# Two transformer blocks on one core: stacked queries and keys in the mixers, a new order of their steps, and row copies by transposes

## The chip, the core and the metric

The kernel runs on one core of one Trainium2 chip. The metric is the device time of one execution in microseconds (us). TensorE (PE in the rows) multiplies 128x128 weight blocks with moving data, VectorE (DVE) and ScalarE (ACT) work element by element, SyncE (SP) issues the loads. Two kernels whose times differ by less than about 0.2% (5 us) can't be told apart by the measurement here.

## The reference

256 tokens of width 1024, float32, pass through a first block of two layers (neighbourhood attention, grouped attention, feed-forward) and a second block of two layers (feed-forward, hybrid mixer, feed-forward). The change is mostly in the hybrid mixer:

```python
def hybrid_mixer(h, ...):
    (q_a, k_a, v_a, f_a, q_b, k_b, v_b, q_c, c_kv, q_i, k_i, w_i, gates) = jnp.split(h @ w_in, _split_points(), axis=-1)
    y_a = forgetting_attention(...)        # 6 "fox" heads of width 64
    y_b = stick_breaking_attention(...)    # 5 "stick" heads
    y_c = dsa_attention(...)               # 5 heads on the 64 best keys of a query, by an index score
    g_a, g_b, g_c = jnp.split(jax.nn.sigmoid(gates), N_BRANCH, axis=-1)
    merged = (g_a * (y_a @ w_up_fox) + g_b * (y_b @ w_up_sb) + g_c * (y_c @ w_up_dsa))
    return merged @ w_out
```

The stick heads need a sum over all later keys before their exponent, so a head is a chain: score, log terms, a second product, exponent, product with the values. The index score of a query goes through relu and a weighted sum, and its 64 largest keys are kept.

## The kernel before, in words

Activations stand transposed: features on the 128 partitions, 256 tokens along the columns. Every float32 operand is split into a high part (`hi`, an ACT instruction of L403) and a low part (`lo`, DVE, L408 or L409), and a product is three matmuls: high by high, high by low, low by high. Nearly all of them are issued at L427. Weights come in by SyncE in pieces of 512 KB, and each piece is split into `hwmx` and `lwmx` (mixers), 512 columns to a buffer, in eight pairs of buffers. The scheduler of the language turns the program into one fixed order for each engine; each engine works through its own in that order and waits where an operand isn't there.

The mixers' program order is a table, `MIX_ORDER`. `K` makes the keys, queries and values that all heads share; `S0` to `S2` and `F0` to `F2` are the projections of the stick and fox heads; `s0` to `s4`, `x0` to `x5` and `d0` to `d5` are the heads; `T0` and `T1` score the index keys of a query block and find the 64 best (eight rounds of MAX and MATCH_REPLACE on DVE, L1568 and L1569); `G` tokens are the gates' projections, `A`, `B` and `C` the ways up (`mix_up`) for fox, stick and dsa heads.

A head is 64 wide, and so are the contractions of its scores: `scores` (L731, fox and dsa heads and the index) and the first products of `stick_head` (L1647) multiply operands on 64 partitions. In the profile a matmul of 64 rows reads `64*128`, one of 128 rows `128*128`. The last of the three chunks of `B` and `C` is 64 rows, too (`n = HD`):

```python
for n, (a, b) in enumerate(((0, 0), (0, 1), (1, 0))):
    nc.tensor.matmul(out, q[a], k[b], start=start and n == 0, stop=stop and n == 2, skip_group_check=True)
```

`rows` (L542) and `b1_keys` (L928) bring a column or row of numbers onto all partitions by a float32 matmul with the identity. `sums` (L486) uses a transpose for a like step.

Of the kernel before, what the change touches and what calls it, by code (L numbers as in the profile page):

```python
# [8 lines left out]
F32 = mybir.dt.float32  # L9
# [113 lines left out]
def _h(base, *hs):  # L123
# [13 lines left out]
MIX_ORDER = (  # L137
    "K S0 T0 F0 s0 s1 S1 T1 S2 s2 s3 G1 G10 x0 F2 F1 s4 G4 G8 x2 G5 B3 x3 d2 G0 d0 G2 G11 x1 d1 G9 x4 x5 d3 d4 d5 A0 G7 B2 G3 B1".split()
)
# [54 lines left out]
def pieces(n, kparts):  # L194

    most = RAW // n // (SUB // n) * (SUB // n)
    return [min(most, nk - k) for nk in kparts for k in range(0, nk, most)]
# [169 lines left out]
class Builder:  # L367
# [171 lines left out]
    def rows(self, ps, r):  # L539

        for t in range(2):
            i = self.nc.tensor.matmul(  # L542
                ps[:, t * P : (t + 1) * P], r[:, t : t + 1].broadcast_to((P, P)), self.ident, start=True, stop=True
            )
        return i
# [157 lines left out]

    def stack_q(self, src, n, scale=1.0):


        t = self.ap_.tile([P, 2, n], F32R, tag="q2", name=self.u("q2"), bufs=2)
# [18 lines left out]

    def scores(self, out, q, k, start=True, stop=True):

        nc = self.nc
        for n, (a, b) in enumerate(((0, 0), (0, 1), (1, 0))):  # L730
            nc.tensor.matmul(out, q[a], k[b], start=start and n == 0, stop=stop and n == 2, skip_group_check=True)  # L731

# [181 lines left out]
    def b1_keys(self, l, w, full, cos, sin):  # L914
# [11 lines left out]
        for t in range(4):  # L926
            o = slice(t * P, (t + 1) * P)
            nc.tensor.matmul(pr[:, o], rw[:, o], self.ident, start=True, stop=True)  # L928
        nc.vector.tensor_tensor(kc, kc, pr, ALU.mult)
# [342 lines left out]
    def mixer(self, l):  # L1272
        w = Weights(self, f"wmx_{l}")
        hh, hl = self.h
        rsb = self.rsb[0]
        xs = lambda k: (hh[:, k], hl[:, k])
        with self.open(f"mo{l}") as op:
            yh = op.tile([P, 9, SEQ], F32R, name=f"yh2{l}")
            yl = op.tile([P, 9, SEQ], F32R, name=f"yl2{l}")
            gates = {}  # L1280
            with self.open(f"ma{l}", "right") as self.ap_:
                run = self.mix_attention(l, w, hh, hl, xs, rsb, yh, yl, op, gates)
            with self.open(f"mm{l}") as mp:
                self.mix_merge(w, run, mp, gates, self.p(f"gf2{l}"))
        assert w.off == w.ap.shape[0] and w.i == len(w.spec)
# [34 lines left out]
    def mix_attention(self, l, w, hh, hl, xs, rsb, yh, yl, op, gates):  # L1320
# [23 lines left out]
        for b in (b1, b2):  # L1344
            t = self.t2("rq")
            self.rope(pairs(t), pairs(b), twice(cr), twice(sr), SWAP2)
            h, lo = self.parts("cq", t, bufs=2)
            qs += [(h[:, :SEQ], lo[:, :SEQ]), (h[:, SEQ:], lo[:, SEQ:])]

# [32 lines left out]
        def query(n, cols):  # L1382

            o = slice(64 * ((n + 1) % 2), 64 * ((n + 1) % 2) + 64)
            return [a[o, cols] for a in qs[(n + 1) // 2]], o

# [4 lines left out]
        def keys(_):  # L1391
# [25 lines left out]
            self.rope(kv[64:, SEQ:], kv[64:, SEQ:], cos[64:], sin[64:], SWAP2)  # L1417
            qs[0] = self.parts("iq", kv[:, SEQ:], SEQ, bufs=1)

        def project(kind, n):  # L1420
            (b,) = self.product()
            wk = w.next()
            if kind == "S" and n == 2:
                self.group([(0, b[:, :SEQ], 0, P, None)], wk, range(NKT), xs)
                k4 = self.t2("k4")[:64, :SEQ]
                nc.scalar.copy(k4, b[64:, :SEQ])
                kt = [ap.tile([64, SEQ], F32R, tag=f"k{c}", name=self.u("k4"), bufs=3) for c in "hl"]
                self.hi(kt[0], k4)
                self.lo(kt[1], k4, kt[0])
                ready[kind, n] = self.parts("q", b[:, :SEQ], SEQ, HD**-0.5, bufs=3), kt  # L1430
                return
            self.group([(0, b[:, :SEQ], 0, P, None), (0, b[:, SEQ:], P, P, None)], wk, range(NKT), xs)
            ready[kind, n] = (
                self.parts("q", b[:, :SEQ], SEQ, HD**-0.5, bufs=3), self.parts("k", b[:, SEQ:], SEQ, bufs=3)
            )
# [5 lines left out]
        def out(i):  # L1441
            if i not in y32:
                y32[i] = ap.tile([P, SEQ], F32, tag="y32", name=self.u("y32"), bufs=3)
            return y32[i]

        def stick(h):
            q, k = ready["S", h // 2]
            o = slice(64 * (h % 2), 64 * (h % 2) + 64)
            y = out(3 + h // 2)
            self.stick_head(h, [a[o] for a in q], [a[o] for a in k], vs, y[o])  # L1450
            if h % 2 or h == 4:
                finish(3 + h // 2, y, P if h % 2 else HD)

        def fox(h):
            i, j = divmod(h, 2)
            if j == 0:
                ck[i] = self.forget_rows(ccol, h)
            q, k = ready["F", i]
            o = slice(64 * j, 64 * j + 64)
            y = out(i)  # L1460
            self.fox_head(h, [a[o] for a in q], [a[o] for a in k], vs, ck[i], j, y[o])
            if j:
                finish(i, y, P)
# [6 lines left out]
        def dsa(n):  # L1470
            hp, qb = divmod(n, 2)
            heads = DSA_HEADS[hp]
            y = out(6 + hp)
            self.dsa_pair(heads, qb, query, vs, masks[qb], y)
            if qb:
                finish(6 + hp, y, len(heads) * HD)
# [33 lines left out]
    def mix_up(self, w, b, yh, yl, g):  # L1510
# [4 lines left out]
        for k in range(3):  # L1515
            n = HD if (b and k == 2) else P
            wh, wl = wk(k)
            for a, y in ((wh, yh), (wh, yl), (wl, yh)):
                for j in range(2):
                    ops.append((0, j, bk[:, j * SEQ : (j + 1) * SEQ], a[:n, j * P : (j + 1) * P], y[:n, 3 * b + k]))  # L1520
        self.matmuls(ops)
# [25 lines left out]
    def index(self, qb, query, ik, fw):  # L1547
# [4 lines left out]
        for hp in range(2):  # L1552
            s = self.bank("s")
            for j in range(2):
                q, o = query(hp + 2 * j, slice(qb * P, (qb + 1) * P))
                self.scores(s[:, j * SEQ : j * SEQ + nk], q, [a[o, :nk] for a in ik])
            rl = self.t2("rl").rearrange("p (a t) -> p a t", a=2)
# [80 lines left out]
    def stick_head(self, h, q, k, vs, y32):  # L1638
# [34 lines left out]
    def dsa_pair(self, heads, qb, query, vs, mask, y32):  # L1673
# [136 lines left out]
```

## Time and profile before

| | us |
|---|---|
| median of 3 runs | 2501.16 (2499.57 to 2503.38) |
| the profiled execution | 2499.92 |
| its span, first to last instruction | 2498.1 |
| PE busy | 2440.1 (98%) |
| DVE busy | 1836.9 (74%) |
| ACT busy | 1373.1 (55%) |

The mixers run from about 1441 to 1682 us and from 2058 to 2300 us of the span. Durations of matmuls overlap: two that follow one another start 0.12 us apart at 256 columns though each lasts 0.28 us. What a matmul costs is therefore read from starts in the timeline, not from durations; the same holds for DVE, to a smaller degree.

### The profile page before, as it was taken

Reading aid. Unit: us, or ns where it says so; the run is one execution under the profiler, and the core shown is the slowest. Engines: PE = TensorE matmul, PEld = TensorE weight load, DVE = VectorE, ACT = ScalarE, POOL = GpSimd, SP = SyncE. Lnnn points to the kernel's source line nnn. Section 1 sums busy time; section 2 is a strip of 40 time slices with the busy share of each in tenths; the row PEclk is TensorE's granted clock in tenths of the full one; section 3 lists DMA queues with packets and bytes.
Section 4 is the critical chain, followed back from the end, with each engine's and each line's share of the span. In section 5 each row is a group of like instructions: output and inputs, shape, how many; then the busy total and the mean of one; then the engine's idle time right before and its main releaser. Section 6 shows DMA issues by size and latency. Waiting matters only on the chain.

```text
span 2498.1 us, 46101 instructions
## 1 busy us (share of the span) xinstructions
PE 2440.1 (98%) x17342; PEld 2257.4 (90%) x17342; DVE 1836.9 (74%) x4131; ACT 1373.1 (55%) x2683; POOL 0.2 (0%) x4
## 2 busy tenths in 40 slices
PE   8999999999999999999999999999999999999997
PEld 4877768888888898999999999999999999999997
DVE  6677886885766889876676687786666668778665
ACT  5566763422233667665555566755555556665553
POOL 0000000000000000000000000000000000000000
PEclk9999999999999999999999999999999999999999
DMA  7221453454654433565555553356666655336553
GB/s 265 92 72 56 147 178 137 159 184 141 208 183 135 127 115 106 155 187 182 182 185 182 184 182 109 113 178 186 181 186 186 183 180 184 100 116 190 184 180 102
DMA packets 112543, 393.46 MB, mean 157 GB/s; under 512 B 12480, under 2 KB 13760, under 8 KB 111808
## 3 DMA queue, kind: packets, MB, share of 16 engines
q1 hardware_dynamic: 112320, 390.52, 49.1%
q8 instruction: 136, 2.23, 0.4%
q14 instruction: 87, 0.71, 0.1%
HBM read 389.42 MB, written 1.05 MB: 156 GB/s over the span
## 4 chain that ended last, share of the span: by engine, by line
PE 95%; DVE 3%; ACT 2%; issue 0%; DMA 0%; SPq 0%; DVEq 0%; ACTq 0%
PE mm L427 84%; PE y L427 2%; PE s L427 2%; PE s L778 1%; PE y L785 1%; PE s L731 1%; PE y L542 1%; PE y L486 0%; PE mm L610 0%; PE y L678 0%; ACT nt L575 0%; DVE lwmx L408 0%; ACT k L403 0%; DVE kl L408 0%; DVE lwm L408 0%
## 5 line engine op out<-in xcount | busy, mean ns | idle before, releaser
L427 PE MATMUL mm<-hh,hwb 128*128 128x512 f32 (+2 forms) x1176 | 348.5, 341 | 2.6 <-ACT gt L1008 1.4
L427 PE MATMUL mm<-hl,hwb 128*128 128x512 f32 (+1 forms) x1176 | 347.5, 340 | 0.1
L427 PE MATMUL mm<-hh,lwb 128*128 128x512 f32 (+2 forms) x1176 | 347.0, 340 | 0.0
L403 ACT ACTIVATE hwb<-wb_0r 128x512 fp32r<-128x512 f32 (+1 forms) x250 | 149.6, 611 | 253.0 <-PE mm L427 243.5
L427 PE MATMUL mm<-gh,hwf 128*128 128x256 f32 x1344 | 269.5, 281 | 0.0
L427 PE MATMUL mm<-gh,lwf 128*128 128x256 f32 x1344 | 269.1, 281 | 0.0
L427 PE MATMUL mm<-gl,hwf 128*128 128x256 f32 x1344 | 268.4, 281 | 0.0
L408 DVE TENSOR_TENSOR lwf<-wf_1r,hwf 128x512 fp32r<-128x512 f32 (+1 forms) x272 | 183.4, 676 | 109.1 <-ACT hwf L403 100.1
L408 DVE TENSOR_TENSOR lwf<-wf_0r,hwf 128x512 fp32r<-128x512 f32 (+1 forms) x272 | 183.3, 675 | 102.9 <-ACT hwf L403 93.1
L403 ACT ACTIVATE hwf<-wf_1r 128x512 fp32r<-128x512 f32 (+1 forms) x272 | 168.2, 619 | 162.9 <-PE mm L427 149.3
L403 ACT ACTIVATE hwf<-wf_0r 128x512 fp32r<-128x512 f32 (+1 forms) x272 | 168.2, 619 | 162.2 <-PE mm L427 146.5
L427 PEld LDWEIGHTS mm<-hh,hwb 128*128 128x128 f32 x1176 | 204.0, 189 | 29.0 <-ACT gt L1008 2.4
L408 DVE TENSOR_TENSOR lwb<-wb_0r,hwb 128x512 fp32r<-128x512 f32 (+1 forms) x250 | 163.4, 665 | 86.2 <-ACT hwb L403 83.3
L427 PEld LDWEIGHTS mm<-hl,hwb 128*128 128x128 f32 x1176 | 203.7, 189 | 25.5 <-DVE hl L408 0.7
L427 PEld LDWEIGHTS mm<-hh,lwb 128*128 128x128 f32 x1176 | 204.1, 189 | 25.0
L403 ACT ACTIVATE hwb<-wb_1r 128x512 fp32r<-128x512 f32 (+1 forms) x242 | 146.2, 611 | 112.2 <-PE mm L427 101.6
L427 PEld LDWEIGHTS mm<-gh,hwf 128*128 128x128 f32 x1344 | 206.4, 188 | 0.0
L427 PEld LDWEIGHTS mm<-gh,lwf 128*128 128x128 f32 x1344 | 206.4, 188 | 0.0
L427 PEld LDWEIGHTS mm<-gl,hwf 128*128 128x128 f32 x1344 | 206.1, 188 | 0.0
L408 DVE TENSOR_TENSOR lwb<-wb_1r,hwb 128x512 fp32r<-128x512 f32 (+1 forms) x242 | 158.3, 666 | 63.2 <-ACT hwb L403 60.1
L427 PE MATMUL mm<-gl,hwmx 128*128 128x256 f32 x656 | 138.9, 289 | 3.3 <-DVE gl L408 3.3
L427 PE MATMUL mm<-actl,hwf 128*128 128x256 f32 x704 | 141.8, 283 | 0.0
(414 smaller groups left out, 5680.9 us busy)
## 6 DMA issues: line engine op xcount, KB each, us to landing
wf_0r<-in_wf_dram SPq DMA_DIRECT2D x120, 512.0 KB, 3.6
wf_1r<-in_wf_dram SPq DMA_DIRECT2D x120, 512.0 KB, 3.5
wb_0r<-in_wb_dram SPq DMA_DIRECT2D x108, 512.0 KB, 3.7
wb_1r<-in_wb_dram SPq DMA_DIRECT2D x105, 512.0 KB, 3.6
wmx_0r<-in_wmx_dram SPq DMA_DIRECT2D x49, 512.0 KB, 3.6
wmx_1r<-in_wmx_dram SPq DMA_DIRECT2D x49, 512.0 KB, 3.6
wm2r<-in_wm_dram SPq DMA_DIRECT2D x48, 512.0 KB, 3.5
wm1r<-in_wm_dram SPq DMA_DIRECT2D x24, 512.0 KB, 4.0
```

Source lines behind the costliest of these rows:

```text
L403: self.nc.scalar.activation(out, src, AF.Copy, scale=scale)
L408: return self.nc.vector.tensor_tensor(out, src, h, ALU.subtract)
L427: i = nc.tensor.matmul(out, lhsT, rhs, start=bank not in first, stop=n[bank] == 0, skip_group_check=True)
L542: i = self.nc.tensor.matmul(ps[:, t * P : (t + 1) * P], r[:, t : t + 1].broadcast_to((P, P)), self.ident, start=True, stop=True)
L731: nc.tensor.matmul(out, q[a], k[b], start=start and n == 0, stop=stop and n == 2, skip_group_check=True)
L778: nc.tensor.matmul(s[:, :nk], q[:, o], part, start=n == 0, stop=n == 1, skip_group_check=True)
L785: nc.tensor.transpose(tp[:, j * P : (j + 1) * P], pt[:, j * P : (j + 1) * P], self.ident)
```

## The change

Stacked scores: the query's high part goes on one half of the partitions and its low part on the other half; the key's high part is written to both halves of one buffer, its low part to both halves of another. A score is then two matmuls of 128 rows. The last chunk of `B` and `C` is multiplied over all 128 rows, and the unused half of `yh` and `yl` is set to zero once a mixer. `rows` and `b1_keys` call a transpose. `MIX_ORDER` is new: both `T` stand ahead of the stick heads, `G8` and `G9` earlier, and `B3` behind `x0` and ahead of `G5`. `out` tells a head whether it is the last of its chunk, so that heads can come in any order. The limits on buffers of queries and keys are 3 and 5.

```diff
--- before.py
+++ after.py
@@ -135,7 +135,7 @@
-    "K S0 T0 F0 s0 s1 S1 T1 S2 s2 s3 G1 G10 x0 F2 F1 s4 G4 G8 x2 G5 B3 x3 d2 G0 d0 G2 G11 x1 d1 G9 x4 x5 d3 d4 d5 A0 G7 B2 G3 B1".split()
+    "K S0 G8 T0 T1 F0 s0 S2 s1 S1 G1 G9 s3 G10 F1 s2 s4 x0 B3 G5 x2 G4 x1 d1 F2 x3 d0 G2 G0 G11 x4 x5 d2 d3 B1 G7 G3 d4 d5 A0 B2".split()
...
@@ -539,9 +539,7 @@
         for t in range(2):
-            i = self.nc.tensor.matmul(
-                ps[:, t * P : (t + 1) * P], r[:, t : t + 1].broadcast_to((P, P)), self.ident, start=True, stop=True
-            )
+            i = self.nc.tensor.transpose(ps[:, t * P : (t + 1) * P], r[:, t : t + 1].broadcast_to((P, P)), self.ident)
...
@@ -724,11 +722,27 @@
-    def scores(self, out, q, k, start=True, stop=True):
+    def stacked_q(self, out, src, a):
+        b = slice(64 - a.start, 128 - a.start)
+        self.hi(out[a], src[a])
+        self.lo(out[b], src[a], out[a])
+    def stacked_k(self, src, a, n):
+        b = slice(64 - a.start, 128 - a.start)
+        h, l = (self.ap_.tile([P, n], F32R, tag=f"k{c}", name=self.u(f"k{c}"), bufs=5) for c in "hl")
+        self.hi(h[a], src[a])
+        self.hi(h[b], src[a])
+        self.lo(l[a], src[a], h[a])
+        self.lo(l[b], src[a], h[a])
+        return h, l
+    def scores(self, out, q, k):
...
-        for n, (a, b) in enumerate(((0, 0), (0, 1), (1, 0))):
-            nc.tensor.matmul(out, q[a], k[b], start=start and n == 0, stop=stop and n == 2, skip_group_check=True)
+        for n, part in enumerate(k):
+            nc.tensor.matmul(out, q, part, start=n == 0, stop=n == 1, skip_group_check=True)
@@ -925,7 +939,7 @@
-            nc.tensor.matmul(pr[:, o], rw[:, o], self.ident, start=True, stop=True)
+            nc.tensor.transpose(pr[:, o], rw[:, o], self.ident)
@@ -1277,6 +1291,10 @@
+            for i in (5, 8):
+                for t in (yh, yl):
+                    self.nc.vector.tensor_copy(t[HD:, i], self.ident[HD:, 0:1].broadcast_to((HD, SEQ)))
@@ -1344,8 +1362,10 @@
-            h, lo = self.parts("cq", t, bufs=2)
-            qs += [(h[:, :SEQ], lo[:, :SEQ]), (h[:, SEQ:], lo[:, SEQ:])]
+            q = ap.tile([P, 2, 512], F32R, tag="cq", name=self.u("cq"), bufs=2)
+            for j in range(2):
+                self.stacked_q(q[:, j], t, slice(64 * j, 64 * j + 64))
+            qs += [q[:, :, :SEQ], q[:, :, SEQ:]]
...
@@ -1415,23 +1434,23 @@
-            qs[0] = self.parts("iq", kv[:, SEQ:], SEQ, bufs=1)
+            qs[0] = ap.tile([P, 2, SEQ], F32R, tag="iq", name=self.u("iq"), bufs=1)
+            self.stacked_q(qs[0][:, 1], kv[:, SEQ:], slice(64, 128))
...
-                k4 = self.t2("k4")[:64, :SEQ]
-                nc.scalar.copy(k4, b[64:, :SEQ])
-                kt = [ap.tile([64, SEQ], F32R, tag=f"k{c}", name=self.u("k4"), bufs=3) for c in "hl"]
-                self.hi(kt[0], k4)
-                self.lo(kt[1], k4, kt[0])
-                ready[kind, n] = self.parts("q", b[:, :SEQ], SEQ, HD**-0.5, bufs=3), kt
+                q = ap.tile([P, 2, SEQ], F32R, tag="q2", name=self.u("q4"), bufs=3)[:, 0]
+                self.hi(q[:64], b[:64, :SEQ], HD**-0.5)
+                self.lo(q[64:], b[:64, :SEQ], q[:64], HD**-0.5)
+                ready[kind, n] = [q], [self.stacked_k(b[:, :SEQ], slice(64, 128), SEQ)]
...
+            q = self.stack_q(b[:, :SEQ], SEQ, HD**-0.5, bufs=3)
...
-                self.parts("q", b[:, :SEQ], SEQ, HD**-0.5, bufs=3), self.parts("k", b[:, SEQ:], SEQ, bufs=3)
+                [q[:, j] for j in range(2)], [self.stacked_k(b[:, SEQ:], slice(64 * j, 64 * j + 64), SEQ) for j in range(2)]
@@ -1439,27 +1458,29 @@
         def out(i):
-            if i not in y32:
-                y32[i] = ap.tile([P, SEQ], F32, tag="y32", name=self.u("y32"), bufs=3)
-            return y32[i]
+            if i in y32:
+                return y32.pop(i), True
+            y32[i] = ap.tile([P, SEQ], F32, tag="y32", name=self.u("y32"), bufs=3)
+            return y32[i], i == 5
...
-            y = out(3 + h // 2)
-            self.stick_head(h, [a[o] for a in q], [a[o] for a in k], vs, y[o])
-            if h % 2 or h == 4:
-                finish(3 + h // 2, y, P if h % 2 else HD)
+            y, last = out(3 + h // 2)
+            self.stick_head(h, q[h % 2], k[h % 2], vs, y[o])
+            if last:
+                finish(3 + h // 2, y, P if h < 4 else HD)
...
-            if j == 0:
-                ck[i] = self.forget_rows(ccol, h)
+            if i not in ck:
+                ck[i] = self.forget_rows(ccol, 2 * i)
...
-            y = out(i)
-            self.fox_head(h, [a[o] for a in q], [a[o] for a in k], vs, ck[i], j, y[o])
-            if j:
+            y, last = out(i)
+            self.fox_head(h, q[j], k[j], vs, ck[i], j, y[o])
+            if last:
...
@@ -1513,11 +1534,10 @@
-            n = HD if (b and k == 2) else P
...
-                    ops.append((0, j, bk[:, j * SEQ : (j + 1) * SEQ], a[:n, j * P : (j + 1) * P], y[:n, 3 * b + k]))
+                    ops.append((0, j, bk[:, j * SEQ : (j + 1) * SEQ], a[:, j * P : (j + 1) * P], y[:, 3 * b + k]))
...
@@ -1644,7 +1664,7 @@
         for b, (o, kb, qs) in enumerate(((z[:, :SEQ], slice(0, P), slice(0, SEQ)), (z[:, SEQ:W], slice(P, SEQ), slice(P, SEQ)))):
-            ops += [(0, b, o, k[i][:, kb], q[j][:, qs]) for i, j in ((0, 0), (0, 1), (1, 0))]
+            ops += [(0, b, o, a[:, kb], q[:, qs]) for a in k]
...
```

On PE a fox head's score stood in the middle of a gate's projection like this (`s` is the score's bank, `mm` the projection):

```order
L427 MATMUL mm1928_18352<-gl1718_16112,hwmx_0_15_0_18334 128x256
L731 MATMUL s1893_18026<-kh1820_17536,qh1818_17532 128x128
L731 MATMUL s1893_18026<-kl1821_17537,qh1818_17532 128x128
L731 MATMUL s1893_18026<-kh1820_17536,ql1819_17533 128x128
L731 MATMUL s1893_18026<-kh1820_17536,qh1818_17532 128x256
L731 MATMUL s1893_18026<-kl1821_17537,qh1818_17532 128x256
L731 MATMUL s1893_18026<-kh1820_17536,ql1819_17533 128x256
L427 MATMUL mm1928_18352<-gl1718_16112,hwmx_0_15_0_18334 128x256
```

and now (L745 is the new line of `scores`):

```order
L427 MATMUL mm1944_18519<-gl1718_16112,hwmx_0_17_0_18501 128x256
L745 MATMUL s1911_18312<-kh1833_17664,q21832_17659 128x128
L745 MATMUL s1911_18312<-kl1834_17665,q21832_17659 128x128
L745 MATMUL s1911_18312<-kh1833_17664,q21832_17659 128x256
L745 MATMUL s1911_18312<-kl1834_17665,q21832_17659 128x256
L427 MATMUL mm1944_18519<-gl1718_16112,hwmx_0_17_0_18501 128x256
L427 MATMUL mm1944_18519<-gh1717_16111,lwmx_0_17_0_18502 128x256 x2
L427 MATMUL mm1944_18519<-gh1717_16111,hwmx_0_17_0_18501 128x256
```

Six matmuls became four, and they are as high as their neighbours.

On PE, while the first stick heads of the first mixer are under way, the program before has a projection (`mm`) around their matmuls (L1663 is a head's second product):

```order
L427 MATMUL mm1926_18281<-gh1717_16111,hwmx_0_14_4_18273 128x256
L1663 MATMUL s1867_17792<-ph1870_17807,stickr1740_16778 128x256
L1663 MATMUL s1867_17792<-ph1870_17807,stickr1741_16780 128x128
L1663 MATMUL s1867_17792<-ph1870_17807,stickr1740_16778 128x128
L427 MATMUL mm1926_18281<-gh1717_16111,hwmx_0_14_4_18273 128x256
L427 MATMUL mm1926_18281<-gl1718_16112,hwmx_0_14_4_18273 128x256
L1663 MATMUL s1867_17792<-pl1871_17808,stickr1740_16778 128x256
L1663 MATMUL s1867_17792<-pl1871_17808,stickr1741_16780 128x128
L1663 MATMUL s1867_17792<-pl1871_17808,stickr1740_16778 128x128
L427 MATMUL mm1926_18281<-gl1718_16112,hwmx_0_14_4_18273 128x256
L427 MATMUL mm1926_18281<-gh1717_16111,lwmx_0_14_4_18274 128x256 x2
L427 MATMUL mm1926_18281<-gh1717_16111,hwmx_0_14_4_18273 128x256 x2
```

Now, from the end of the projection of `F1` on, 32 rows hold matmuls of stick heads alone; these are the last of them and what comes next. `mm1924` is the way up `B3`, which reads `yh`, the finished output of the first two heads, and `mm1925` is the gate `G5`:

```order
L427 MATMUL y1858_17785<-ph1856_17781,vs21756_17025 128x256
L427 MATMUL y1858_17785<-pl1857_17782,vs21756_17025 128x256
L427 MATMUL y1858_17785<-ph1856_17781,vs21756_17025 128x128
L427 MATMUL y1858_17785<-pl1857_17782,vs21756_17025 128x128
L1683 MATMUL s1871_18024<-ph1874_18037,stickr1740_16782 128x256
L1683 MATMUL s1871_18024<-ph1874_18037,stickr1741_16784 128x128
L1683 MATMUL s1871_18024<-ph1874_18037,stickr1740_16782 128x128
L1683 MATMUL s1871_18024<-pl1875_18038,stickr1740_16782 128x256
L1683 MATMUL s1871_18024<-pl1875_18038,stickr1741_16784 128x128
L1683 MATMUL s1871_18024<-pl1875_18038,stickr1740_16782 128x128
L427 MATMUL mm1924_18358<-yh20_16769,hwmx_0_15_0_18350 128x256 x2
L427 MATMUL mm1925_18398<-gh1717_16111,hwmx_0_16_0_18380 128x256 x2
```

The projection that could be done meanwhile now stands behind a matmul that needs the heads.

On DVE, between the low part that the first head's second product reads (`pl1842`, which stands two rows ahead, with one weight split between) and the one that its product with the values reads (`pl1844`), there now stand the end of one search (`sc1803`), the beginning of the other (`sc1817`), weight splits and the doubled low keys (`kl`):

```order
L1588 MAX small1814_17536<-sc1803_17498 128x8
L408 TENSOR_TENSOR kl1863_17870<-mm1860_17795,kh1862_17869 64x256 x2
L408 TENSOR_TENSOR lwmx_0_16_6_18395<-wmx_0r3975168_18388,hwmx_0_16_6_18394 128x512
L1589 MATCH_REPLACE sc1803_17498<-small1814_17536,sc1803_17498 128x128
L408 TENSOR_TENSOR lwmx_0_17_0_18502<-wmx_0r4106240_18499,hwmx_0_17_0_18501 128x512
L408 TENSOR_TENSOR kl1865_17876<-mm1860_17795,kh1864_17875 64x256 x2
L1588 MAX small1815_17539<-sc1803_17498 128x8
L1588 MAX small1822_17564<-sc1817_17544 128x8
L1589 MATCH_REPLACE sc1803_17498<-small1815_17539,sc1803_17498 128x128
L408 TENSOR_TENSOR lwmx_0_17_2_18506<-wmx_0r4106240_18499,hwmx_0_17_2_18505 128x512
L1589 MATCH_REPLACE sc1817_17544<-small1822_17564,sc1817_17544 128x256
L408 TENSOR_TENSOR pl1844_17702<-zm1839_17684,ph1843_17701 128x384
```

Before, the search of the second query block came behind the first two heads. The program as a whole has 80 fewer matmuls in the two mixers (40 of 128 columns, 40 of 256), and DVE has in each mixer 33 low parts of 64x256 and 4 of 64x512 more, 12 of 128x256 and 2 of 128x512 fewer, and 4 fills of zeros. The order of the first block moved too, by neighbouring steps changing places.

## Rows read from the trace of the kernel before

**Rows 1.** Chain that ended last, its engines; span and clock of the core.
```profile
PE 95%; DVE 3%; ACT 2%; issue 0%; DMA 0%; SPq 0%; DVEq 0%; ACTq 0%
...
core 0: 2498.1 us, clock 0.989
```

**Rows 2.** First mixer in two windows: us, then busy us of each engine, clock, DMA.
```profile
1440.00:1560.00 120.00, 115.80 (x860) 111.51 (x860) 97.81 (x261) 73.98 (x160) 0.00 (x0) 0.96 0.46 146
1560.00:1680.00 120.00, 119.31 (x955) 114.01 (x954) 95.30 (x244) 79.43 (x182) 0.00 (x0) 1.00 0.46 142
```

**Rows 3.** Timeline of PE, first mixer: start, us from first to last end, form.
```profile
1544.81 0.40 PE L427 MATMUL mm<-gh,hwmx 128*128 128x256 f32 x2
1545.05 0.28 PE L427 MATMUL mm<-gl,hwmx 128*128 128x256 f32 x1
1545.26 0.32 PE L731 MATMUL s<-kh,qh 64*128 64x128 f32 x1
1545.42 0.27 PE L731 MATMUL s<-kl,qh 64*128 64x128 f32 x1
1545.53 0.27 PE L731 MATMUL s<-kh,ql 64*128 64x128 f32 x1
...
1546.14 0.38 PE L427 MATMUL mm<-gl,hwmx 128*128 128x256 f32 x1
1546.36 0.28 PE L427 MATMUL mm<-gh,lwmx 128*128 128x256 f32 x1
```

**Rows 4.** Timeline of PE at two score blocks that stand side by side.
```profile
1600.00 0.32 PE L731 MATMUL s<-kh,qh 64*128 64x128 f32 x1
...
1601.16 0.39 PE L427 MATMUL y<-ph,vs 128*128 128x256 f32 x1
```

**Rows 5.** Timeline of PE at L542 and L486; counts of L542 and L928.
```profile
1238.53 0.38 PE L486 MATMUL y<-const,sq 128*128 128x128 f32 x2
1238.67 0.36 PE L427 MATMUL mm<-acth,hwb 128*128 128x256 f32 x1
...
1451.30 0.61 PE L542 MATMUL y<-const,rcol 128*128 128x128 f32 x4
1451.66 0.36 PE L427 MATMUL mm<-gh,lwmx 128*128 128x256 f32 x1
...
L542 PE MATMUL y<-const,rcol x76: 270/275/551, 21.4 to 2490.3; 128*128 128x128 f32 x76
...
L542 PE MATMUL y<-const,ccol x48: 270/275/324, 1555.1 to 2221.1; 128*128 128x128 f32 x48
...
L928 PE MATMUL y<-const,rw x16: 270/275/275, 78.4 to 859.6; 128*128 128x128 f32 x16
```

**Rows 6.** Windows of the first mixer in which the granted clock was half.
```profile
1515.90:1519.30 3.40, 3.40 (x17) 3.40 (x17) 2.44 (x8) 1.52 (x4) 0.00 (x0) 0.50 0.10 12
1533.00:1539.80 6.80, 6.80 (x28) 6.11 (x29) 6.24 (x19) 4.47 (x12) 0.00 (x0) 0.50 0.00 1
```

**Rows 7.** Timeline of DVE, first mixer: starts give the pitch of each form.
```profile
1528.96 0.69 DVE L408 TENSOR_TENSOR lwmx<-wmx_0r,hwmx 128x512 fp32r<-128x512 f32 x1 [1.47 <-ACT hwmx L403]
1529.57 0.55 DVE L408 TENSOR_TENSOR pl<-ze,ph 128x384 fp32r<-128x384 f32 x1
...
1534.87 0.42 DVE L408 TENSOR_TENSOR k<-k,k 64x256 fp32r<-64x256 f32 x1 [0.30 <-ACT k L403]
1535.32 0.42 DVE L764 TENSOR_TENSOR y<-y,yt 64x256 f32<-64x256 f32 x1
...
1537.91 0.42 DVE L1568 MAX8 small<-sc 128x8 f32<-128x256 f32 x1
1538.25 0.54 DVE L408 TENSOR_TENSOR pl<-ze,ph 128x384 fp32r<-128x384 f32 x1
1538.70 0.08 DVE L1569 MATCH_VALUE_LOAD sc<-small,sc 128x8 f32 x1
...
1539.10 0.41 DVE L408 TENSOR_TENSOR kl<-mm,kh 128x256 fp32r<-128x256 f32 x1
```

More of the change, by code (lines that the diff above doesn't have):

```diff
@@ L194, in pieces @@
 def pieces(n, kparts):
-    most = RAW // n // (SUB // n) * (SUB // n)
+    most = max(RAW // n // (SUB // n) * (SUB // n), 1)
     return [min(most, nk - k) for nk in kparts for k in range(0, nk, most)]
@@ L702, in parts, with stack_q @@
         return h, l
-    def stack_q(self, src, n, scale=1.0):
-        t = self.ap_.tile([P, 2, n], F32R, tag="q2", name=self.u("q2"), bufs=2)
+    def stack_q(self, src, n, scale=1.0, bufs=2):
+        t = self.ap_.tile([P, 2, n], F32R, tag="q2", name=self.u("q2"), bufs=bufs)
         for j in range(2):
@@ L1382, in query @@
         def query(n, cols):
-            o = slice(64 * ((n + 1) % 2), 64 * ((n + 1) % 2) + 64)
-            return [a[o, cols] for a in qs[(n + 1) // 2]], o
+            return qs[(n + 1) // 2][:, (n + 1) % 2, cols]
         self.tc.keep_in_program_order(nc.scalar.preload_act_table_set("natural_log_exp_and_others"))
@@ L1472, in dsa @@
             heads = DSA_HEADS[hp]
-            y = out(6 + hp)
+            y, last = out(6 + hp)
             self.dsa_pair(heads, qb, query, vs, masks[qb], y)
-            if qb:
+            if last:
                 finish(6 + hp, y, len(heads) * HD)
@@ L1554, in index @@
             for j in range(2):
-                q, o = query(hp + 2 * j, slice(qb * P, (qb + 1) * P))
-                self.scores(s[:, j * SEQ : j * SEQ + nk], q, [a[o, :nk] for a in ik])
+                q = query(hp + 2 * j, slice(qb * P, (qb + 1) * P))
+                self.scores(s[:, j * SEQ : j * SEQ + nk], q, [a[:, :nk] for a in ik])
             rl = self.t2("rl").rearrange("p (a t) -> p a t", a=2)
@@ L1618, in fox_head @@
             self.scores(
-                s[:, qb * SEQ : qb * SEQ + n], [a[:, qb * P : (qb + 1) * P] for a in q], [a[:, :n] for a in k]
+                s[:, qb * SEQ : qb * SEQ + n], q[:, qb * P : (qb + 1) * P], [a[:, :n] for a in k]
             )
@@ L1678, in dsa_pair @@
         for j in range(n):
-            q, o = query(4 + heads[j], slice(qb * P, (qb + 1) * P))
-            self.scores(s[:, j * SEQ : j * SEQ + nk], q, [a[o, :nk] for a in self.ck_])
+            q = query(4 + heads[j], slice(qb * P, (qb + 1) * P))
+            self.scores(s[:, j * SEQ : j * SEQ + nk], q, [a[:, :nk] for a in self.ck_])
         pt = self.t2("pt")
```

## The prediction

> **What bounds the kernel now.** I read three views first: the chain of work that ended last, the windows of the mixers, and the timeline of PE. The reader should see in the chain that 95% of it is PE, and in the windows that PE was busy 115.80 and 119.31 of 120 us in the two halves of a mixer, DVE 97.81 and 95.30, ACT 73.98 and 79.43 [rows 1, 2]. So the time is what PE does, plus what little it waits: 4.2 + 0.7 = 4.9 us a mixer. The second mixer's halves agree with the first's within 0.3 us. A change is worth the time that it takes out of PE's stream or the waits that it puts in.
>
> **Term 1: the change of height.** In an undisturbed stream a matmul of 256 columns costs 0.12 us (two from 1544.81 to 1545.05), and one of 128 columns 0.11 (1545.42 to 1545.53). Around a score block of 64 rows it is otherwise: from the neighbour at 1545.05 to the next but one at 1546.36 eight matmuls start in 1.31 us, where 5 at 0.118 and 3 at 0.11 make 0.92 [rows 3]. The 0.39 us too much lie ahead of the first (0.21 instead of 0.12), inside (six in 0.88 instead of 0.68), and behind the block (0.22 instead of 0.12). I went through PE's timeline for all such blocks: 68, 34 a mixer, from the index scores near 1506 to the ways up near the mixer's end. Their excess is 31.9 us; 3.4 of it are waits and 2.8 lie under the half clock, which leaves 25.7, or 0.38 a block. The change leaves no 64-row matmul in the mixers (336 before: 240 of scores, 96 of ways up), so the whole falls away: **−25.7 us**. Below that I see no reason to go; 128-row matmuls from other heads stand in the same stream at 0.11 to 0.12.
>
> A rule of the Trainium skill speaks against this edit: TensorEngine Tiling (Array Packing), section Theoretical Speedup, lets a contraction of up to 64 rows run up to twice as fast, since two halves of the array work at once. By it the 240 score products before would have cost 13.7 us less, and the forecast below would be that much higher. The trace shows such a pair only where two heads' blocks stand side by side: twelve products from 1600.00 to 1601.16, where 1.37 would be their sum [rows 4], once a mixer.
>
> **Term 2: products taken out.** Three score products become two: 80 fewer in the program, 40 of 256 and 40 of 128 columns, at 0.118 and 0.11: **−9.1 us**. The ways up keep their number of matmuls and columns, so more rows in them cost nothing on PE.
>
> **Term 3: rows by transposes.** Two float32 products at L542 leave four matmul records, and hold PE from 1451.30 to 1451.66, 0.36 us; two transposes at L486 hold it from 1238.53 to 1238.67, 0.14 [rows 5]. That is 0.112 us for each of 70 (76 + 48 + 16 records, two each): **−7.8 us**, 3.6 of it in the mixers.
>
> **Term 4: what DVE and ACT get.** Stacking takes two instructions of 64 partitions where one of 128 did. DVE: 33 more of 64x256 and 4 fills at 0.42, 4 of 64x512 at 0.69 as for full height, less 12 of 128x256 at 0.42 and 2 of 128x512 at 0.69: +12 us a mixer busy, on 193 of some 230. By pitch they weigh more, since a 64x256 part costs 0.45 to the next start [rows 7] and a 128x256 one less, about the 0.34 of a MAX over as many columns: +14. ACT gains about 10 on 153. The cover is that both idle while PE streams weights. It holds in the second half, where nothing but weight splits and softmax heads stand; there I cost the work at nothing. In the first half two places lose it.
>
> At the shared queries (`cq`, the fills) DVE has about 3 us more (four parts of 64x512 for two of 128x512, four fills) ahead of `gl`, the low part of the activations, which every projection needs. I added up pitches of DVE's rows and of PE's rows in their orders from the mixer's first weight split on. Before, DVE's sum never passes PE's by over 0.6 us; now it passes it by 3.9 at the `gl` products of `S0`.
>
> At the stick heads, from behind `pl1842` to `pl1844`, DVE has four weight splits at 0.61 us, four low keys at 0.45, three MAX at 0.34, three replaces with their load at 0.40 and the `pl` at 0.45 [rows 7]: 6.9 us. PE has 1.7 us of work meanwhile. On to the addition that completes the first two heads, DVE has six MAX, five replaces, five 384-wide steps at 0.45, three of 64x256 at 0.45 and a mask, 7.9 more, 14.8 in all; PE's rows up to `B3`, which waits for just that, are 4.6: 12 of 256 columns, 20 of 128, and eight around the projection's end. PE could wait 10.2 us. By the running sums DVE comes there about 5 us ahead, so 5.1 are left, and 9.0 in the mixer. Behind `B3` the gate `G5` and then `x2` wait too, since PE takes its rows in order. Chains of ACT and DVE add to this, as before (4.9 us waited where the sums ask for 0.6): I take 11.5 us a mixer, +6.6, **+13 us** in both. The lower end is +0, if DVE's lead is larger than pitches from before tell; the upper is all of 3.9 + 10.2 with 3 us of chains, 17, or +24.
>
> **The clock.** Two stretches of the first mixer run at 1.2 GHz, granted clock 0.50, 3.4 and 6.8 us long [rows 6], behind the index scores and the first stick heads, where PE had waited; the second mixer has the same two. They cost 5.1 us a mixer. New waits stand at the same place, so I leave this term at zero; its ends are −10 (all four gone) and +10 (as much again).
>
> **The sum.** 2499.9 − 25.7 − 9.1 − 7.8 + 13 = 2470 us, against the profiled execution; that one lies 1.2 below the median of the three runs, within their spread, so I don't correct for it. 5 us, 0.2%, is about what a measurement can tell from no change.
>
> **The rivals.**
> - A, as above: 2462 to 2478, chance 0.52.
> - B, the new waits are hidden: DVE comes to the stick heads with 10 us of lead, as idle time of 22 us in the first half would allow [rows 2], and the denser stream lifts the clock in some of the four stretches. 2499.9 − 42.6 = 2457, and 2447 with all four gone. For it: DVE's rows don't depend on PE while they search. Against it: searches begin only once the index scores are there. Chance 0.22.
> - C, DVE arrives with no lead: +24, and the clock stays low for the 15 us in which PE only waits and does heads, +0 to +6: 2481 to 2488. For it: PE ran dry here before as well. Chance 0.20.
> - D, the height isn't what costs 0.39 us, but the change of a bank or of an accumulation in the middle of another; then four products in place of six pay it too. 2499.9 − 9.1 − 7.8 + 13 = 2496, at the edge of no change. Against it: `y` products of 128 rows stand in the same streams without it. Chance 0.03.
> - E, slower: DVE becomes the bound of a mixer's first half. Its 22 us of idle time there are waits for data that stay, and all 14 us by pitch come on top of the 120: then both first halves take 14 more instead of about 9 less, and only the second halves' share (19 us) and the rows outside the mixers (4) are gained: 2499.9 + 28 − 23 = 2505. It decides from 17 us more waiting a mixer than I forecast. Chance 0.02.
> - F, the clock falls with the transposes. They would have to bring a stretch like the 3.4 us one, 1.7 us lost, at 20 of their 35 pairs to eat up the gain: 2504 and more. Against it: L486 has 52 such pairs before, and a mean clock of 0.989 [rows 1] is 55 us at the half clock in all, where 52 such stretches would be 177. Chance 0.01. This is what the Trainium skill's TensorE: Matmul & The Clock Gate, Part 4: PE-mode transpose, would let one fear, since by it transposes don't count as busy work for the clock; the trace, with its 55 us, does not bear it out.
>
> **How the numbers follow.** The time is A's, 2470. The range 2450 to 2488 holds A, C and the upper half of B: 0.52 + 0.20 + 0.12, 0.84. Faster by over 0.2% are A, B and C, 0.94; same D, 0.03; slower E and F, 0.03.
>
> **What would show it.** Term 1: no gap of 0.21 us around scores in the profile after, and four of them start in 0.46. Term 3: two rows by transpose in 0.14 us. Term 4: waits of PE for `gl` of some 4 us around `S0`, for `pl` or `ph` behind `F1`, and for `yh` or `yl` at `B3`, together 9 to 14 us a mixer, all in the first half; the second half shorter by about 9 us with under 1 us of waits. I am wrong if scores keep a gap, if PE's waits stay near 5 us (B), or if DVE is busy without a break for longer than the 15 us at the stick heads (C, E).

## The result, and the profile after

The changed kernel takes **2474.05 us** (median of 4 runs, 2473.95 to 2475.28), the one before 2502.08 beside it: a ratio of 0.989, with an interval of 0.9873 to 0.9907. The forecast was 2470, with a range of 2450 to 2488. The span went from 2498.1 to 2471.8, by 26.3 us; 4.2 of it lie outside the mixers, 10.6 in the first mixer and 11.5 in the second.

The answers to [rows 1] are the chain that ended last, by engine,

```profile
PE 90%; DVE 6%; ACT 2%; issue 1%; DMA 0%; SPq 0%; DVEq 0%; ACTq 0%
```

and to [rows 2] the first mixer's two stretches (us, then busy us of PE, weight load, DVE, ACT and POOL, then clock and DMA):

```profile
1437.00:1557.00 120.00, 112.53 (x852) 109.71 (x851) 104.36 (x271) 84.35 (x178) 0.00 (x0) 0.94 0.47 146
1557.00:1667.00 110.00, 108.36 (x913) 107.40 (x912) 98.80 (x261) 78.33 (x187) 0.00 (x0) 1.00 0.51 156
```

PE's part of the chain fell from 95% to 90%, DVE's rose from 3% to 6%, and ACT's stayed at 2%: DVE now ends more of the waits. In the first stretch PE is busy for 112.53 us of 120, where it was 115.80, and DVE for 104.36, where it was 97.81.

The answer to [rows 3] is a fox head's score in the timeline of PE (start, length, form):

```profile
1550.52 0.28 PE L427 MATMUL mm<-gl,hwmx 128*128 128x256 f32 x1
1550.64 0.22 PE L745 MATMUL s<-kh,q 128*128 128x128 f32 x1
1550.70 0.27 PE L745 MATMUL s<-kl,q 128*128 128x128 f32 x1
1550.81 0.33 PE L745 MATMUL s<-kh,q 128*128 128x256 f32 x1
1550.98 0.28 PE L745 MATMUL s<-kl,q 128*128 128x256 f32 x1
1551.10 0.28 PE L427 MATMUL mm<-gl,hwmx 128*128 128x256 f32 x1
```

From the neighbour at 1550.52 to the score is 0.12 us, and the four products take 0.46 to the start of the next projection matmul. No gap is left.

What PE waited for in the first mixer (engine, line, for whom; us, times, longest):

```profile
PE s L1683 <- ACT ph L403: 1.7, 2, 1.1
PE mm L427 <- DVE gl L408: 1.6, 1, 1.6
PE y L427 <- DVE pl L408: 1.4, 1, 1.4
PE mm L427 <- DVE lwmx L408: 1.0, 1, 1.0
PE s L745 <- ACT pt L769: 0.8, 1, 0.8
PE s L427 <- DVE kl L408: 0.8, 1, 0.8
PE mm L427 <- DVE gate L1542: 0.7, 2, 0.5
PE s L427 <- ACT zm L1684: 0.6, 1, 0.6
PE s L1683 <- DVE pl L408: 0.3, 1, 0.3
```

Together 8.9 us, where it was 4.9; in the second mixer 9.6, where it was 4.8. In the timeline five of these rows stand at the stick heads, between the end of `F1` and `B3`, and make 4.7 us:

```profile
1528.07 0.38 PE L427 MATMUL s<-q,kl 128*128 128x256 f32 x1 [0.76 <-DVE kl L408]
...
1530.43 0.38 PE L427 MATMUL y<-pl,vs 128*128 128x256 f32 x1 [1.42 <-DVE pl L408]
...
1532.05 0.90 PE L1683 MATMUL s<-ph,stickr 128*128 128x256 f32 x3 [1.07 <-ACT ph L403]
...
1534.48 0.58 PE L427 MATMUL s<-q,kh 128*128 128x256 f32 x1 [0.58 <-ACT zm L1684]
...
1537.48 0.90 PE L1683 MATMUL s<-ph,stickr 128*128 128x256 f32 x3 [0.61 <-ACT ph L403]
1538.69 0.90 PE L1683 MATMUL s<-pl,stickr 128*128 128x256 f32 x3 [0.30 <-DVE pl L408]
1539.58 0.79 PE L427 MATMUL mm<-yh,hwmx 128*128 128x256 f32 x2
```

The last row is `B3`: it did not wait, though by little, since ACT's `yh` ended at 1539.53. The other waits are `lwmx` at 1463.8 (1.0, new) and `gl` at 1475.8 (1.6, as before), and 1.5 in the mixer's second half (`pt` and `gate`).

To compare kernels below I added up, for both mixers, the gaps between starts of PE's matmuls beyond their pitch, by kind: at a change of height, in stretches at the half clock, and the rest over 0.12 us, which are waits (more than the profile's list has, where a matmul that still runs counts as busy). Two small transposes of 64 rows a mixer stand in all of these kernels and are not counted.

| kernel | both mixers, us | gaps of height | waits | half clock |
|---|---|---|---|---|
| before | 477.8 | 26.6 | 11.7 | 6.0 |
| changed | 455.7 | 0 | 26.3 | 6.8 |
| rows_alone | 473.1 | 25.5 | 11.7 | 5.8 |
| order_alone | 484.5 | 24.6 | 15.6 | 9.0 |
| old_order | 467.9 | 0 | 37.4 | 8.4 |
| low_two | 469.5 | 20.7 | 21.8 | 5.4 |
| up_alone | 468.4 | 18.2 | 10.9 | 5.6 |
| three_products | 465.3 | 0 | 25.4 | 7.7 |
| half_search | 469.5 | 0 | 37.6 | 8.4 |
| kl_on_act | 468.4 | 0 | 36.9 | 8.9 |
| g5_filled | 468.6 | 0 | 36.5 | 7.6 |
| g5_early | 472.9 | 0 | 40.2 | 10.0 |
| t1_later | 486.1 | 0 | 44.2 | 17.6 |
| fills_act | 455.1 | 0 | 25.5 | 7.6 |

### The profile page after: what moved, and what is told of

The parts are those of the page before. It is cut to its first block, busy times and chain, and to the rows that moved or that the text cites. A ratio compares the mean times of both kernels' runs of the same rounds, so it can differ in the third digit from the quotient of the medians.

```text
span 2471.8 us, 45879 instructions
## 1 busy us (share of the span) xinstructions
PE 2404.3 (97%) x17192; PEld 2234.2 (90%) x17192; DVE 1856.1 (75%) x4185; ACT 1391.2 (56%) x2731; POOL 0.2 (0%) x4
## 4 chain that ended last, share of the span: by engine, by line
PE 90%; DVE 6%; ACT 2%; issue 1%; DMA 0%; SPq 0%; DVEq 0%; ACTq 0%
PE mm L427 82%; PE y L427 2%; PE s L427 1%; PE s L792 1%; PE y L799 1%; DVE lwmx L408 1%; PE s L745 1%; ACT pt L769 1%; DVE lwm L408 0%; PE y L486 0%; PE y L676 0%; DVE kl L408 0%; DVE ptl L408 0%; DVE small L758 0%; PE y L542 0%
## 5 line engine op out<-in xcount | busy, mean ns | idle before, releaser
L427 PE MATMUL mm<-acth,hwf 128*128 128x256 f32 x704 | 141.8, 283 | 0.0
```

The costliest lines, as they stand in the source:

```text
L427: i = nc.tensor.matmul(out, lhsT, rhs, start=bank not in first, stop=n[bank] == 0, skip_group_check=True)
```

## The experiments

My theory was the forecast's: height costs 0.38 us a block, products and row copies cost their pitch, and the new order with DVE's added work puts new waits at the stick heads. The rivals: the gaps come from something else (D), the clock falls with the transposes (F), and, for the waits, that a head's own chain of steps is what PE waits for, not DVE's sum of work. All ratios are to the kernel before.

**Row copies alone.**

```diff
 (before)
-            i = self.nc.tensor.matmul(
-                ps[:, t * P : (t + 1) * P], r[:, t : t + 1].broadcast_to((P, P)), self.ident, start=True, stop=True
-            )
+            i = self.nc.tensor.transpose(ps[:, t * P : (t + 1) * P], r[:, t : t + 1].broadcast_to((P, P)), self.ident)
...
-            nc.tensor.matmul(pr[:, o], rw[:, o], self.ident, start=True, stop=True)
+            nc.tensor.transpose(pr[:, o], rw[:, o], self.ident)
```

> The kernel before with transposes in rows and b1_keys, and nothing else. If 70 row copies cost 0.112 us less each, 7.8 us less than before: about 2494, 4.2 of it outside the mixers. If transposes let the clock fall (rival F), more half-clock stretches than before's and a time of 2500 or more. If the copies are hidden behind waits, under 4 us less.

2490.32, ratio 0.9956 (0.9944 to 0.9969): 11.0 us less, 3 more than expected. In the profiled execution (2488.25, the shortest of five) the mixers are 4.7 shorter, against 3.6. Part of the rest is the clock: before the first mixer this execution had 13.6 us at 1.2 GHz, the one of before 23.8, and the changed kernel, with the same first block, 20.4. F is out: the granted clock was 0.992 in this execution and 0.989 to 0.992 in the five, where it was 0.988 to 0.990 before.

**Height alone**, on the changed kernel:

```diff
 (changed)
-            nc.tensor.matmul(out, q, part, start=n == 0, stop=n == 1, skip_group_check=True)
+            nc.tensor.matmul(out, q[:64], part[:64], start=n == 0, stop=n == 1, skip_group_check=True)
...
-            ops += [(0, b, o, a[:, kb], q[:, qs]) for a in k]
+            ops += [(0, b, o, a[:64, kb], q[:64, qs]) for a in k]
```

> The changed kernel with its two products a score on 64 partitions instead of 128 (the halves above are left out of the sums; all instructions stay, DVE and ACT work too). If the height costs 0.38 us a block, the 52 score blocks cost 20 us: about 2494, with starts 0.2 us apart around them. If it is the change of bank or of accumulation (rival D), no difference to the changed kernel, 2474.

2486.95, ratio 0.9942 (0.9927 to 0.9958): 12.9 us more than the changed kernel. The order of this kernel's instructions is the changed kernel's, row for row, on PE, DVE and ACT; only the height differs. Its fox score in the timeline:

```profile
1551.95 0.28 PE L427 MATMUL mm<-gl,hwmx 128*128 128x256 f32 x1
1552.16 0.33 PE L745 MATMUL s<-kh,q 64*128 64x128 f32 x1
1552.32 0.27 PE L745 MATMUL s<-kl,q 64*128 64x128 f32 x1
1552.43 0.33 PE L745 MATMUL s<-kh,q 64*128 64x256 f32 x1
1552.61 0.27 PE L745 MATMUL s<-kl,q 64*128 64x256 f32 x1
1552.81 0.39 PE L427 MATMUL mm<-gl,hwmx 128*128 128x256 f32 x1
1553.03 0.40 PE L427 MATMUL mm<-gh,lwmx 128*128 128x256 f32 x2
```

0.21 ahead, 0.65 for four instead of 0.46, 0.22 behind: 0.39 us, the same sum as in [rows 3], with four products in place of six. D is out. The gaps sum to 20.7 us, as expected; PE's other waits are 4.5 us shorter, since what PE loses to height it need not wait for DVE and ACT later, and the half clock costs 1.4 less. That is why only 13 of the 20 show.

**Ways up alone**: the kernel before, with the last chunk over 128 rows and the four fills.

```diff
 (before)
+            for i in (5, 8):
+                for t in (yh, yl):
+                    self.nc.vector.tensor_copy(t[HD:, i], self.ident[HD:, 0:1].broadcast_to((HD, SEQ)))
...
-            n = HD if (b and k == 2) else P
...
-                    ops.append((0, j, bk[:, j * SEQ : (j + 1) * SEQ], a[:n, j * P : (j + 1) * P], y[:n, 3 * b + k]))
+                    ops.append((0, j, bk[:, j * SEQ : (j + 1) * SEQ], a[:, j * P : (j + 1) * P], y[:, 3 * b + k]))
```

> The kernel before with the last chunk of the ways up over 128 rows and the four fills a mixer, and nothing else. If height alone costs 0.39 us a block, the 20 blocks of ways up are worth 7.8 us: about 2494. If the fills or the clock eat it, 2498 to 2503.

2491.10, ratio 0.9957 (0.9942 to 0.9972): 10.4 less; gaps of height fell by 8.4, with 22 runs of 64-row matmuls fewer (46 instead of 68). The same matmuls over twice the rows are faster, because they no longer change the height.

**The third product.**

```diff
 (changed)
-        for n, part in enumerate(k):
-            nc.tensor.matmul(out, q, part, start=n == 0, stop=n == 1, skip_group_check=True)
+        for n, part in enumerate((*k, k[1])):
+            nc.tensor.matmul(out, q, part, start=n == 0, stop=n == 2, skip_group_check=True)
...
-            ops += [(0, b, o, a[:, kb], q[:, qs]) for a in k]
+            ops += [(0, b, o, a[:, kb], q[:, qs]) for a in (*k, k[1])]
```

> The changed kernel with three products of 128 rows a score again (the low key's product is made twice, so that the scores are off by its size). If a product costs its pitch and no more, 80 matmuls at 0.118 and 0.11 bring 9.1 us back: 2483. If PE's waits for heads cover part of them (they stand in the stretch where PE waits for DVE), 3 to 7 us: 2477 to 2481.

2482.11, ratio 0.9920 (0.9904 to 0.9937): 8.1 more than the changed kernel, 9.6 in the mixers. A product costs its pitch.

**The order alone, and the stacking with the old order.**

```diff
 (before; "out" and the heads' last step as in the change)
-    "K S0 T0 F0 s0 s1 S1 T1 S2 s2 s3 G1 G10 x0 F2 F1 s4 G4 G8 x2 G5 B3 ...
+    "K S0 G8 T0 T1 F0 s0 S2 s1 S1 G1 G9 s3 G10 F1 s2 s4 x0 B3 G5 x2 G4 ...
```

> The kernel before with the new order of steps alone (and the bookkeeping that lets heads come in any order). If it is the order that puts the waits at the stick heads, the mixers get 3 to 6 us longer each and the time is 2507 to 2514, with PE waiting between the end of F1 and B3. If the waits come from the stacking's work on DVE, the order alone changes less than 3 us either way.

2506.48, ratio 1.0021 (1.0012 to 1.003): 5 us more, about the least that can be told from no change, and between the two outcomes expected. Its added waits are not where they were expected: the largest is for a gate's bank behind `B3` (2.5 us in the first mixer, 1.1 in the second), and of the 6.7 us in the mixers 3.0 are the half clock. The reverse edit on the changed kernel:

> The changed kernel with the order of before. If the new order causes the added waits, this one is faster than the changed kernel, 2460 to 2468. If the added work on DVE causes them and the new order is what makes room for it, it is slower than the changed kernel, 2478 to 2490. If neither, 2472 to 2476.

2485.47, ratio 0.9938 (0.9924 to 0.9951), 11.4 us **slower** than the changed kernel. The order costs 5 us where heads are made of 64-row products, and saves 11 where they are stacked. With the old order PE has three waits that the new one avoids, 6.3 us in its first mixer:

```profile
PE y L1649 <- DVE pt L772: 3.4, 1, 3.4
...
PE mm L427 <- ACT gate L1529: 1.9, 1, 1.9
...
PE mm L427 <- ACT gate L1508: 1.0, 1, 1.0
```

The 3.4 us are a fox head with nothing beside it. `gate L1529` is a bank: a gate behind `s4` leaves its product in one of three banks until its tanh, and the tanh is held behind the last logarithm of the stick heads. `gate L1508` is a bank, too, of an earlier gate that ACT copies out.

**Is it DVE that the stick heads wait for?** Three edits, on the changed kernel: half of each search, the second copy of the low keys on ACT, and a projection put back among the heads.

```diff
 (half_search)
-        for _ in range(8):
+        for _ in range(4):
 (kl_on_act)
-        self.lo(l[b], src[a], h[a])
+        self.nc.scalar.copy(l[b], l[a])
 (g5_filled; G4 copied out and its tanh taken from the copy)
-    "K S0 ... s4 x0 B3 G5 ...
+    "K S0 ... s4 x0 G5 B3 ...
...
-            if late is None:
+            if late is None and n != 4:
...
-                late.append(g)
+                if late is None:
+                    self.tanh(g, g)
+                else:
+                    late.append(g)
...
-            if t == "s4":
+            if t == "G5":
```

> The changed kernel with four rounds of each search instead of eight (it keeps 32 keys of a query where the reference keeps 64). That takes 5.8 us a mixer from DVE, nearly all of it between the first head's second product and B3. If DVE's row of work there is what PE waits for, PE's waits at the stick heads fall by 3 to 5 us a mixer and the time to 2464 to 2468. If a head's own chain is the wait, they stay and the time is 2472 to 2475.

> The changed kernel with the second half of each stacked low key copied by ACT from the first half, instead of computed again on DVE: 11 of 64x256 a mixer leave DVE (5 us by pitch), 11 come to ACT. If DVE is the bound at the stick heads, 2 to 4 us less a mixer: 2466 to 2470. If ACT's own chain or the copy's place in it is the bound, 2473 to 2478.

> The changed kernel with G5 ahead of B3, and with the gates G5 and G4 copied out of their banks at once, so that no bank waits for the tanh behind the last head. A projection then stands among the stick heads again. If PE's waits there come from having nothing else to do, they fall by 3 us or more a mixer: 2466 to 2470. If DVE's sum of work up to B3 is the bound, the waits only move and the time stays 2472 to 2478.

2486.22, 2484.91 and 2485.50; ratios 0.9936 (0.9922 to 0.9951), 0.9931 (0.9916 to 0.9946) and 0.9937 (0.992 to 0.9954). By the expectations each was to be faster or up to 4 us slower; each is 11 to 12 us slower. The first tells most. The stretch of the stick heads, in the changed kernel and then with half the search (columns as above), and PE's waits there with half the search:

```profile
1526.50:1540.00 13.50, 8.70 (x38) 7.03 (x37) 12.94 (x40) 8.25 (x19) 0.00 (x0) 0.68 0.25 78
```

```profile
1526.50:1540.00 13.50, 8.77 (x42) 7.64 (x41) 9.96 (x25) 9.03 (x21) 0.00 (x0) 0.69 0.24 79
```

```profile
1527.98 0.39 PE L427 MATMUL s<-q,kh 128*128 128x256 f32 x1 [0.94 <-ACT zm L1684]
1529.09 0.38 PE L427 MATMUL s<-q,kl 128*128 128x256 f32 x1 [0.72 <-DVE kl L408]
...
1530.61 0.39 PE L427 MATMUL y<-pl,vs 128*128 128x256 f32 x1 [0.62 <-DVE pl L408]
...
1532.15 0.90 PE L1683 MATMUL s<-ph,stickr 128*128 128x256 f32 x3 [0.98 <-ACT ph L403]
...
1534.27 0.58 PE L427 MATMUL s<-q,kh 128*128 128x256 f32 x1 [0.58 <-ACT zm L1684]
...
1537.54 0.90 PE L1683 MATMUL s<-ph,stickr 128*128 128x256 f32 x3 [0.88 <-ACT ph L403]
```

DVE is busy for 9.96 us instead of 12.94, with a hole of 2.35 us (ahead of a `pl` at 1535.04, which waited for ACT), and PE still waits 4.7 us. So work taken from DVE took nothing off the wait. It doesn't follow that DVE's row wasn't the cause in the changed kernel. There the chain that ended last goes over DVE's rows alone from 1521.8 on, and leaves them for the first time behind a `pl` at 1532.5 (start, length, what):

```profile
1532.49 0.47 DVE pl L408
...
1533.00 0.91 PE s L1683 x3
...
1533.94 0.49 ACT zm L1684
```

Of the 4.7 us 3.2 lie ahead of 1533.0. In the second mixer the chain stays with DVE up to 2145.7, the last product ahead of `B3`. With half of each search it leaves DVE earlier:

```profile
1530.10 0.47 DVE pl L408
...
1530.61 0.57 PE y L427 x3
```

From there on it goes over PE and ACT by turns. That is the other thing that can hold a head, its own chain: second product, exponent and high part on ACT, low part on DVE, product with the values, addition, with nothing for PE between the steps. So DVE's row ends last in the changed kernel, and the heads' own chain is about as long: where the one gets shorter, the other holds PE. This is a reading of two traces whose orders differ, since the scheduler moved other steps too. With `G5` among the heads the waits in the stretch fall to 2.9 us, and 1.0 comes back at the next head, at 1561.

What makes all three slower stands behind that stretch: a gate's bank (0.6 to 2.2 us a mixer) and the last dsa heads, 2.3 to 2.4 us, as here in kl_on_act (in g5_filled also 1.7 us ahead of ways up):

```profile
1613.22 0.39 PE L427 MATMUL y<-ph,vs 128*128 128x256 f32 x1 [0.58 <-ACT ph L403]
...
1615.82 0.39 PE L427 MATMUL y<-ph,vs 128*128 128x256 f32 x1 [0.82 <-ACT ph L403]
...
1618.33 0.58 PE L427 MATMUL y<-ph,vs 128*128 128x256 f32 x1 [0.99 <-ACT ph L403]
```

Little else is left for PE there, and the last row is at the half clock (granted 0.50 from 1617.7 on; 0.58 us for one matmul, where the first row has 0.39). The edits did not touch these steps; the scheduler put them elsewhere.

**Moving steps**, on the changed kernel: `G5` ahead of `s4` (`F1 s2 G5 s4 x0 B3 x2`), and `T1` behind it (`K S0 G8 T0 F0 ... F1 s2 s4 T1 x0 B3`).

> The changed kernel with the gate G5 moved ahead of s4 in the order, so that a projection stands where the heads had PE to themselves. If PE waits there because it has nothing else to do while DVE works off the search, the keys and the splits, the 4 to 5 us of waits at the stick heads go: mixers 3 to 5 us shorter each, 2464 to 2468. If DVE is the bound of the stretch whatever PE has to do, the waits move behind G5 and the time stays within 2 us of 2474.

> The changed kernel with the second search T1 behind the stick heads. If the search on DVE is what the heads wait for, their waits fall by 3 us or more a mixer, and the time with them, unless the later search is waited for by the dsa heads: 2466 to 2470. If the chain of a head itself (ACT and DVE steps one after another) is the wait, 2472 to 2480.

2491.20, ratio 0.9954 (0.9939 to 0.9969), and 2502.51, 0.9998 (0.9989 to 1.0007). Both expectations missed. With `G5` early the waits at the heads fall to 3.2 us, but `G4` is the next projection, and the tanhs of five gates stand ahead of its own; ACT in the timeline, and the matmul that waits:

```profile
1558.07 0.61 ACT L1674 ACTIVATE ze<-ze,one 128x384 f32<-128x384 f32 x1
1558.69 1.28 ACT L1529 ACT_TABLE_LOAD   x1
1559.99 2.71 ACT L1529 ACTIVATE gate<-gate 128x512 f32<-128x512 f32 x5
1562.60 0.57 ACT L1529 ACTIVATE gate<-mm 128x512 f32<-128x512 f32 x1
```

```profile
1563.22 0.80 PE L427 MATMUL mm<-gh,hwmx 128*128 128x256 f32 x2 [4.92 <-ACT gate L1529]
```

4.92 us for one bank. With `T1` late five waits of 2.9 us are left at the stick heads instead of 4.7. The first search's last rounds still stand there, up to 1529.3. The chain that ended last leaves DVE's rows at 1528.2 and goes over PE, ACT and DVE by turns, and 2.2 us of the waits lie behind that. So in this order the heads' own chain leaves about 2 us, and 1.9 went with the second search. The waits that come up behind are larger (a gate's bank 3.1, the last heads 3.2), and 24 us a mixer run at the half clock.

**Zeros on ACT**: the four fills as `nc.scalar.copy` instead of `nc.vector.tensor_copy`.

> The changed kernel with the four fills of zeros a mixer on ACT instead of DVE. If DVE's work ahead of the shared low parts is what PE waits for at the mixer's start, the waits for lwmx (1.0) and gl (1.6) shrink by about 1 us a mixer: 2471 to 2473. The scheduler moves other steps too when four instructions change engines; if the changed kernel's time hangs on its very order behind the stick heads, the waits for a gate's bank and at the last dsa heads come up as in the other variants, and the time is 2480 to 2487.

2471.93, ratio 0.9879 (0.9862 to 0.9897): the fastest. Its four runs (2471.63 to 2472.46) lie below all of the changed kernel's, though the intervals overlap. The 1.0 us for `lwmx` is gone, `gl` keeps its 1.6, and here the scheduler's new order did no harm behind the stick heads.

## Why the prediction was right, and where luck helped it

- **Term 1** (−25.7): right. The gaps of height fell by 26.6 us; two experiments gave 0.38 to 0.40 us a run of 64-row matmuls without the rest of the change (8.4 us for 22 in up_alone, 20.7 for 52 in low_two).
- **Term 2** (−9.1): right; 8.1 to 9.6 by its own experiment.
- **Term 3** (−7.8): right as far as it can be read. In the changed kernel four projection matmuls and one transpose of L542 take 0.59 us of PE's starts, from 1448.66 to 1449.25, where the four alone take 0.47: 0.12 a transpose. Before, two products and two projection matmuls took 0.69 us, from 1451.18 to 1451.87: 0.22 a product. Of the 70 products 36 lie in the mixers by their rows, which makes 4.0 there and not 3.6. Outside the mixers 4.2 us were measured, but in eleven executions with the new first block the first mixer began 3.0 to 6.0 us earlier than before, so the clock's part and the term's can't be told apart there.
- **Term 4** (+13): the mechanism is borne out, the size in part by luck. By the profile's list, in which the forecast counted, PE waits 8.8 us more in both mixers (8.9 and 9.6, where 9 to 14 a mixer were named); by the table, which also counts the last matmul ahead of a wait, 14.6 more. At the start, `gl` did not grow to 3.9 us; 1.0 at `lwmx` came in its place, and fills_act takes it away. At the stick heads I priced DVE's work up to `B3`, and the trace bears that out as a duration: from the start of `pl1842` to that of `pl1844` DVE took 6.5 us without a break, to the addition 15.3, where 6.9 and 14.8 were forecast.

```profile
1523.32 0.55 DVE L408 TENSOR_TENSOR pl<-ze,ph 128x384 fp32r<-128x384 f32 x1
...
1529.83 0.55 DVE L408 TENSOR_TENSOR pl<-zm,ph 128x384 fp32r<-128x384 f32 x1
...
1538.66 0.42 DVE L778 TENSOR_TENSOR y<-y,yt 64x256 f32<-64x256 f32 x1
```

 The step that failed is "by the running sums DVE comes there about 5 us ahead, so 5.1 are left". `pl1842` ended at 1523.87, and PE took it up here:

```profile
1525.81 0.45 PE L1683 MATMUL s<-pl,stickr 128*128 128x256 f32 x3
```

 So DVE was 1.9 us ahead, nearer to C's condition than to A's. The wait of 4.7 us is near the 5.1 all the same, because a second number was off the other way: from 1525.81 to `B3` PE took 9.0 us besides the listed waits, and not 4.6. Of the 4.4 us too much, about 2.5 are the half clock by an estimate from pitches (22 of the 40 matmuls ran in it); the rest is the last matmul ahead of each wait. 15.3 − 9.0 − 1.9 is 4.4, as 14.8 − 4.6 − 5 was 5.2: two errors that cancel, which is luck. One of my signs of being wrong came true, too: DVE has no idle time of 0.1 us or more from 1513.6 to 1536.1, longer than the 15 us. The forecast adds the chains of ACT and DVE to DVE's row; the runs show them as a second bound beside it: with half of each search all of the 4.7 us stayed, without the second search 2.9. Also `B3` did not wait for `yh`, as I had said, and the second half has 1.5 us of waits where I forecast under 1.
- **The order.** I took it for the cause of the added waits. Alone it does cost 5 us, but the stacking with the old order waits 11 us more than with the new one. Two edits that each change who is late can't be priced one by one.
- **The clock** (0): right on the sum. The two short stretches became one of 13.7 and one of 10.2 us in the mixers, 6.8 us of cost instead of 6.0.

The sum from the table is −26.6 − 9.1 − 4.0 + 14.6 + 0.8 = −24.3 in the mixers, where 22.1 were measured; 2.2 us stay unassigned. Open is what decides where the scheduler leaves PE without work behind the stick heads: five edits there brought the same two waits and one did not, and none of these six held the order still, as low_two does. So what a shorter row of DVE alone would be worth, with the order held, is not shown.

## What to carry to other kernels

Look at the starts around matmuls of another height, not at their lengths: a short run of them inside a full-height stream cost 0.39 us here, more than the products it saved, and filling the other half of the rows (with zeros, or with the low part) was faster than leaving it out.

When an engine is full at the place where another waits, ask what would hold the other one next. Here the chain that ended last went over DVE's rows, and yet half of the searches taken away left the wait as long, because a head's own chain is about as long. Follow the chain from step to step in both traces before such work is priced.

Where a scheduler sets the order, an edit of a few instructions is an edit of the whole order behind it. Read the waits after the place as well as at it before the edit is judged.

## What the runs showed of the hardware that was not expected

The same part of a program does not always get the same clock. The first block ran with 23.8, 20.4 and 13.6 us at 1.2 GHz before its first mixer in three executions (before; changed; rows_alone), the last two of them on the same instructions in the same order. In the eleven executions with that first block it was 13.6 to 23.8 us, and the first mixer began between 1432.4 and 1435.4 us. That is 3 us, as much as the smaller effects here; what decides it is not shown.
